# First block of two transformer blocks: scores written in alternation between row groups, compression weights used unsplit in column groups, planner given new durations

## The chip, the cores and the metric

The kernel runs on one core of one Trainium2 chip. The metric is device time in microseconds (us), the median of the runs shown; lower is better. The engines are named as in the profile: PE (TensorE; PEld is its weight load), DVE (VectorE), ACT (ScalarE), POOL (GpSimd) and SP (SyncE, which issues the DMAs).

## The reference

Two layers of a first block, then two layers of a second block, on 256 tokens of width 1024, all in fp32. The first block's layer has a sparse attention whose keys and values are, among other things, compressed. What the change touches is this:

```python
def compress(t, pe, w1, b1, w2, b2):            # once for keys, once for values, per layer
    ...
    flat = blocks.transpose(...).reshape(B, nc, G, CMP_LEN * D)     # 15 blocks x 2 groups = 30 rows of 2048
    h = jax.nn.gelu(flat @ w1 + b1)                                 # w1 is 2048 x 256
    return h @ w2 + b2
...
s_s = jnp.einsum('bqgrd,bgqkd->bgrqk', qb, k_g) * scale             # 8 heads of depth 64, in 2 groups of 4
s_w = jnp.einsum('bqgrd,bkgd->bgrqk', qb, kwb) * scale              # the same queries, windowed keys
```

With 256 tokens the selection keeps every block, so selected and windowed attention are both causal attention, with different keys and values. Projections, a gated MLP, a convolutional feed-forward part and the second block (pooling, gated linear attention, latent attention, feed-forward) follow.

## The kernel before

The program is recorded first and emitted afterwards. Every operation goes to a recorder as one `Op`; a list scheduler (`schedule`) then simulates the five engines with the durations of `_cost`, takes at each step the ready operation of lowest priority number, and so fixes the order of every engine's queue. The priority is the position in the program plus a number from the table `SHIFT`, by phase and group; the table `ALT` moves single operations to another engine (a copy from ACT to DVE, an elementwise operation from DVE to POOL and back). On the chip each engine runs its queue in this order and waits on semaphores. Since every operation is emitted from one line (L522 before, L534 after), the profile tells operations apart by tile names: `wh`/`wl` are the two parts of a weight tile, `raw` the tile as it came by DMA, `x` the split activations, `u` general tiles, and `pa`, `pb`, `upp`, `trp` PSUM tiles, two buffers of each, one bank a buffer.

A matmul on large weights is done in three: the weights are split into a rounded part and a remainder (`split`: `wh` by a copy, `wl` by a subtraction), the activations too, and high x high, high x low and low x high are summed in PSUM. Small matmuls (scores, products with the values, transposes) are plain fp32; an fp32 matmul that is not a transpose shows as two instructions, one for each of two passes.

`first_mix(i)` is the first part of a layer. `weave` interleaves generators: `compress_g(kv)` runs beside input projections, `attend_g(t)` (t is the half of the tokens, 128 each) beside the gated MLP's projections and the compressed attention.

- `compress_g`: 16 steps m of 128 rows each. For each it multiplies `xs_[:, m]` (30 columns high, 30 low) by `lv` and `hv`, two matmuls of 256 columns per step, all into one PSUM tile `trp`. Rows 0 to 29 and 30 to 59 of the result are then added by a product with the constant `pair_sum` (60 rows), once for each half of the 256 hidden values.
- `attend_g`: for t = 0 two heads share a PSUM tile `upp` (128 queries x 2 heads x 2 kinds x 128 keys), for t = 1 one head fills it. A head's score has a depth of 64, that is rows 0 to 63 of the array for the first four heads (g = 0) and rows 64 to 127 for the others (g = 1). Behind each score stands a bf16 matmul that adds the causal mask, over all 128 rows.

Of the kernel before, what the change touches and what calls it, by code (L numbers as in the profile page):

```python
# [174 lines left out]
class Recorder:  # L175
# [14 lines left out]

    def mask(self, lz):
# [115 lines left out]
def _cost(eng, meth, args, kw, reads, writes):  # L307
# [209 lines left out]
def emit(nc, order):  # L517
    for op in order:
# [9 lines left out]
        (0, 0): 11, (0, 2): -701  # L528
    },
# [5 lines left out]
    },  # L535
# [5 lines left out]
    },  # L541
    "f1m": {
        (1, 0): -520, (1, 1): -3630, (1, 2): -723, (2, 0): -251, (2, 1): 188, (2, 2): -699
    },
# [11 lines left out]
    },  # L556
# [82 lines left out]
        (0, 0): 76, (0, 2): 156  # L639
    },  # L640
    "s2": {
        (0, 0): 185
    },
}
HOLD = {
# [1366 lines left out]
```

## Time and profile before

| | |
|---|---|
| median of 3 runs (lowest, highest) | 1585.4 us (1585.31, 1591.89) |
| span of the profiled execution | 1583.9 us |
| what lies around the span, by the median | 1.5 us |
| busy: PE, PEld | 1562.3 us (99%), 1358.9 us (86%) |
| busy: DVE, ACT, POOL | 1083.7 us (68%), 761.7 us (48%), 492.3 us (31%) |
| DMA | 270.60 MB, 171 GB/s in the mean |

The page gives for the profiled execution its span, from the first instruction to the last; the time that the runs are measured by is a little longer. A matmul's end is modelled in the profile, so PE's durations overlap; the pace is read from the distance between starts.

### The profile page before, as it was taken

The page shows a single profiled execution, that of the slowest core. Times are in us where ns is not written, and L with a number is a line of the kernel's source. Part 1 is how long each engine was busy: PE and PEld are TensorE (multiplying, and loading weights), DVE is VectorE, ACT ScalarE, POOL GpSimd, SP SyncE. Part 2 cuts the span into 40 slices and gives each one's busy share as a digit, 9 for nine tenths or more (in the row PEclk, how much of TensorE's full clock was granted, in tenths as well). Part 3 has the DMA queues.
Part 4 walks back from the last instruction along what each step waited for, and adds up shares of the span by engine and source line. Part 5 has one row for each costly group of instructions (what it writes and reads, how often), then busy time and mean ns, then how long its engine had stood idle before and what let it go on. Part 6 is the DMA issues. An engine that isn't in the chain of part 4 may idle for free.

```text
span 1583.9 us, 24617 instructions
## 1 busy us (share of the span) xinstructions
PE 1562.3 (99%) x9421; PEld 1358.9 (86%) x9421; DVE 1083.7 (68%) x1582; ACT 761.7 (48%) x1333; POOL 492.3 (31%) x428
## 2 busy tenths in 40 slices
PE   7999999999999999999999999999999999999998
PEld 6778999988778999988888888999988888889997
DVE  6777877888777877886645647566566455675664
ACT  4566555554666545556453444323354534343242
POOL 2433111122433111115233552323443326424233
PEclk9999999999999999999999999999999999999999
DMA  8643765745644656736534556566555344555571
GB/s 271 221 147 103 216 186 176 217 129 172 202 128 129 211 180 189 211 121 194 180 109 132 166 186 193 172 188 188 163 183 186 107 139 160 193 173 174 178 224 38
DMA packets 264091, 270.60 MB, mean 171 GB/s; under 512 B 11698, under 2 KB 196645, under 8 KB 263973
## 3 DMA queue, kind: packets, MB, share of 16 engines
q1 hardware_dynamic: 263972, 269.03, 55.0%
q8 instruction: 74, 1.21, 0.3%
q14 instruction: 45, 0.36, 0.1%
HBM read 267.94 MB, written 1.05 MB: 170 GB/s over the span
## 4 chain that ended last, share of the span: by engine, by line
PE 96%; DVE 2%; ACT 1%; DMA 1%; SPq 0%; issue 0%; POOL 0%; DVEq 0%; POOLq 0%; ACTq 0%
PE pa L522 36%; PE upp L522 35%; PE pb L522 19%; PE trp L522 5%; DMA raw<-in_w_in_dram 1%; DVE wl L522 1%; DVE u L522 1%; SPq L522 0%; ACT L522 0%; ACT u L522 0%; ACT junk L522 0%; DVE x L522 0%; DVE wh L522 0%; ACT x L522 0%; POOL sm L522 0%
## 5 line engine op out<-in xcount | busy, mean ns | idle before, releaser
L522 ACT CAST wh<-raw 128x1024 fp32r<-128x1024 f32 (+3 forms) x382 | 393.0, 1033 | 470.3 <-PE upp L522 234.1
L522 DVE TENSOR_TENSOR wl<-raw,wh 128x1024 fp32r<-128x1024 f32 (+3 forms) x402 | 500.5, 1257 | 119.2 <-ACT wh L522 114.5
L522 PE MATMUL upp<-x,wh 128*128 128x256 f32 x2560 | 479.3, 283 | 0.0
L522 PE MATMUL pa<-wh,x 128*128 128x512 f32 (+1 forms) x1280 | 425.9, 402 | 3.7 <-DVE x L522 2.0
L522 PEld LDWEIGHTS upp<-x,wh 128*128 128x128 f32 x2560 | 406.3, 191 | 6.2 <-ACT wh L522 0.3
L522 PE MATMUL upp<-x,wl 128*128 128x256 f32 x1280 | 361.3, 283 | 1.5 <-DVE wl L522 1.5
L522 POOL TENSOR_TENSOR wl<-raw,wh 128x1024 fp32r<-128x1024 f32 (+2 forms) x94 | 228.7, 2436 | 282.8 <-ACT wh L522 121.7
L522 PEld LDWEIGHTS pa<-wh,x 128*128 128x128 f32 x1280 | 236.7, 189 | 53.2 <-ACT u L522 2.6
L522 PE MATMUL pa<-wl,x 128*128 128x512 f32 (+1 forms) x640 | 251.9, 401 | 0.0
L522 PEld LDWEIGHTS upp<-x,wl 128*128 128x128 f32 x1280 | 244.6, 191 | 3.4 <-DVE wl L522 2.0
L522 POOL TENSOR_TENSOR u<-u,u 128x256 f32<-128x256 f32 (+4 forms) x98 | 109.3, 1117 | 328.0 <-ACT u L522 288.0
L522 DVE CAST wh<-raw 128x1024 fp32r<-128x1024 f32 (+3 forms) x114 | 89.3, 787 | 100.3 <-PE pa L522 38.7
L522 PE MATMUL pb<-wh,x 128*128 128x512 f32 (+2 forms) x496 | 157.4, 384 | 0.0
L522 PEld LDWEIGHTS pa<-wl,x 128*128 128x128 f32 x640 | 120.8, 189 | 21.4 <-DVE u L522 0.8
L522 DVE TENSOR_TENSOR u<-upp,u 128x512 f32<-128x512 f32 x80 | 55.2, 690 | 72.4 <-PE upp L522 71.6
L522 PEld LDWEIGHTS pb<-wh,x 128*128 128x128 f32 x496 | 90.4, 188 | 15.8 <-ACT wh L522 0.6
L522 PE MATMUL pb<-wl,x 128*128 128x512 f32 (+2 forms) x248 | 92.2, 381 | 0.0
L522 PE MATMUL trp<-c_ident,u 128*128 128x128 f32 (+4 forms) x415 | 79.5, 274 | 2.6 <-DMA u<-in_pre_mix_g_dram 1.9
L522 POOL TENSOR_TENSOR sm<-sm,c_nhalf 128x1 f32<-128x1 f32 (+1 forms) x60 | 47.9, 799 | 106.3 <-DVE sm L522 104.3
L522 DVE SCALAR_TENSOR_TENSOR u<-u,c_cols_conv_w,u 128x254 f32<-128x254 f32 (+1 forms) x176 | 73.5, 478 | 0.0
L522 ACT ACTIVATE u<-u 128x256 f32<-128x256 f32 (+1 forms) x100 | 44.5, 445 | 55.5 <-DVE u L522 49.6
L522 POOL TENSOR_TENSOR al<-u,ah 128x256 fp32r<-128x256 f32 x22 | 22.6, 1027 | 148.0 <-ACT ah L522 78.0
(209 smaller groups left out, 2092.3 us busy)
## 6 DMA issues: line engine op xcount, KB each, us to landing
raw<-in_w_in_dram SPq DMA_DIRECT2D x112, 512.0 KB, 4.0
raw<-in_w_up_dram SPq DMA_DIRECT2D x88, 512.0 KB, 4.2
raw<-in_w_ffn_gu_dram SPq DMA_DIRECT2D x88, 512.0 KB, 4.8
raw<-in_w_down_dram SPq DMA_DIRECT2D x44, 512.0 KB, 4.4
raw<-in_w_ffn_down_dram SPq DMA_DIRECT2D x44, 512.0 KB, 4.1
raw<-in_w_o_dram SPq DMA_DIRECT2D x32, 512.0 KB, 4.0
raw<-in_cmp_w_dram SPq DMA_DIRECT2D x16, 512.0 KB, 4.9
raw<-in_w_ple_gate_dram SPq DMA_DIRECT2D x16, 512.0 KB, 3.9
```

Of the source, the lines that this page charges most:

```text
L522: f(*args, **kw)
```

## The change

Four things change in the program, and the order of everything is planned anew.

1. `attend_g` makes two score tiles `SS[0]`, `SS[1]` at a time, one for each g, and writes the scores in the order g = 0, g = 1, for t = 0 twice. The masks of both tiles are written behind them. `rec.together` makes the planner place a score only when both tiles have a bank.
2. `compress_g` no longer splits weights or activations. Step m is one fp32 matmul of 32 columns (30 and two of zeros), with result rows 32r to 32r + 31 for r = m mod 4.
3. The four partial results are added by a `pair_sum` of 128 rows, which is four unit matrices one above the other.
4. `_cost` has other durations for PE; nearly all numbers of `SHIFT` and `ALT` are replaced. Of 496 weight remainders (`wl`), 94 were made on POOL; now there are 480, of which 184 are made on POOL.

```diff
+    def together(self, op, lz):
+        t = lz.tile
+        if t not in op.tiles:
+            op.tiles.append(t)
+            t.ops.append(op)
...
         if meth == "transpose":
-            return 107.0, None
+            return 106.5, None
...
-            d = 2 * max(2 * c / 2.4, 107.0)
+            d = 2 * max(2 * c / 2.4, 107.0) + 2.5
+            if args[1].shape[-1] <= 32 and rhs.shape[0] == 128 and c == 256:
+                d = 130.0
+            elif rhs.shape[0] == 64:
+                d = 2 * c / 2.4 + 110.0
+            elif rhs.shape[0] < 64:
+                d += 190.0
         elif rhs.dtype == F32R:
-            d = c / 2.4 if c >= 256 else 4 * c / 2.4
+            d = c / 2.4 + 10.8 if c >= 256 else 4 * c / 2.4
...
 SHIFT = {
     "c1": {
-        (0, 0): 11, (0, 2): -701
+        (0, 0): -537, (0, 2): -2513
...
-    c["pair_sum"] = np.concatenate([np.eye(30, dtype=f), np.eye(30, dtype=f)], axis=0)
+    c["pair_sum"] = np.concatenate([np.eye(32, 30, dtype=f)] * 4, axis=0)
...
-            xs_ = X4.tile([128, 16, 2, 30])
-            Xm = X[:, :480].rearrange("p (m n) -> p m n", m=16)
-            nc.scalar.copy(xs_[:, :, 0], Xm)
-            nc.vector.tensor_tensor(xs_[:, :, 1], Xm, xs_[:, :, 0].bitcast(F32), op=ALU.subtract)
-            yield
...
-                    hv, lv = split(load(w1[:, m0:m0 + 4]))
-                    for mm in range(4):
-                        m = 8 * mq + 4 * mh + mm
-                        if m > 0:
-                            nc.tensor.matmul(ps1[:30, :256], xs_[:, m, 0], lv[:, mm], start=False, stop=False)
-                        nc.tensor.matmul(ps1[:60, :256], xs_[:, m].rearrange("p a n -> p (a n)"), hv[:, mm],
-                                         start=(m == 0), stop=(m == 15))
...
+            for mq in range(4):
+                raw = load(w1[:, 4 * mq:4 * mq + 4])
+                for r in range(4):
+                    nc.tensor.matmul(ps1[32 * r:32 * r + 32, :256], X[:, 4 * mq + r], raw[:, r], start=(mq == 0),
+                                     stop=(mq == 3))
+                yield
...
-                for e in range(nh):
-                    nc.tensor.matmul(S[:, e], qT[t][gp, j0 + e], kT[gp, :, 0:(t + 1) * 128], start=True, stop=False)
-                    mask_add(S[:, e, :, t * 128:(t + 1) * 128], 2)
...
+            for j0 in range(0, 4, nh):
+                SS = [bank(upp, "S").rearrange("p (e b n) -> p e b n", e=nh, b=2) for g in range(2)]
                 for e in range(nh):
+                    for g in range(2):
+                        gp = slice(g * 64, (g + 1) * 64)
+                        op = nc.tensor.matmul(SS[g][:, e], qT[t][gp, j0 + e], kT[gp, :, 0:(t + 1) * 128],
+                                              start=(e == 0), stop=False, skip_group_check=True)
+                        rec.together(op, SS[1 - g])
+                for g in range(2):
+                    S, h0 = SS[g], 4 * g + j0
+                    for e in range(nh):
+                        mask_add(S[:, e, :, t * 128:(t + 1) * 128], 2, skip_group_check=True)
```

Where the rows stand now is shown at three places. The first is PE's queue at the first scores of the first layer (t = 0). A score is `upp<-u,u 128x256`, a mask `upp<-c_causal_b,c_ident_b`. Before:

```order
L522 MATMUL pa_224<-wh_69,x_78 128x512
L522 MATMUL upp_227<-u_85,u_88 128x256
L522 LDWEIGHTS c_ident_b_196
L522 MATMUL upp_227<-c_causal_b_195,c_ident_b_196 128x256
L522 MATMUL upp_227<-u_85,u_88 128x256
L522 LDWEIGHTS c_ident_b_196
L522 MATMUL upp_227<-c_causal_b_195,c_ident_b_196 128x256
L522 MATMUL upp_228<-u_85,u_88 128x256
```

After, at the same place:

```order
L534 MATMUL pa_224<-wh_66,x_77 128x512
L534 MATMUL upp_227<-u_88,u_87 128x256
L534 MATMUL pa_224<-wl_71,x_77 128x512
L534 MATMUL upp_228<-u_88,u_87 128x256
L534 MATMUL pa_224<-wh_66,x_78 128x512
L534 MATMUL upp_227<-u_88,u_87 128x256
L534 MATMUL upp_228<-u_88,u_87 128x256
L534 LDWEIGHTS c_ident_b_196
L534 MATMUL upp_227<-c_causal_b_195,c_ident_b_196 128x256
```

The masks have moved behind the scores, and two projection matmuls (`pa`) stand between the first three scores; only the third and the fourth follow each other. Over both layers, the 32 scores stood in 32 separate places before, and now stand in 27: five pairs are adjacent (four with 256 columns, one with 512).

The second place is PE's queue at the compression of the keys in the first layer (all four weight pieces of 512 KB). Before, its first piece:

```order
L522 MATMUL pb_226<-wh_66,x_77 128x512
L522 MATMUL trp_230<-wh_67,x_79 60x256
L522 MATMUL trp_230<-wl_72,x_79 30x256 x2
L522 MATMUL trp_230<-wh_67,x_79 60x256
L522 MATMUL trp_230<-wl_72,x_79 30x256
```

After, all four pieces:

```order
L534 MATMUL upp_228<-wh_67,x_75 128x280
L534 MATMUL trp_229<-raw_64,u_84 32x256 x4
L534 MATMUL trp_229<-raw_59,u_84 32x256 x4
L534 MATMUL trp_229<-raw_62,u_84 32x256 x4
L534 MATMUL trp_229<-raw_58,u_84 32x256 x4
L534 MATMUL upp_227<-wl_72,x_75 128x280
```

The 32 matmuls of 60 or 30 columns have become 16 of 32 columns, without a break. For the values there are breaks: in both layers their 16 stand as 8, 1, 1 and 6, with single transposes between.

The third place is the head of SP's queue, the DMA issues in order. Before:

```order
L522 DMA raw_58<-in_w_in_dram 128x2x512
L522 DMA c_ident_190<-const_ident_dram 128x128
L522 DMA c_h_191<-in_x_dram 128x512 x4
L522 DMA u_84<-in_pre_mix_g_dram 16x128
L522 DMA raw_60<-in_w_in_dram 128x2x512
```

After:

```order
L534 DMA raw_58<-in_w_in_dram 128x2x512
L534 DMA w_179<-in_cmp_w_dram 128x2x64
L534 DMA b_181<-in_cmp_b_dram 30x64
L534 DMA raw_59<-in_w_in_dram 128x2x512
L534 DMA c_ident_190<-const_ident_dram 128x128
L534 DMA c_h_191<-in_x_dram 128x512 x4
L534 DMA u_85<-in_pre_mix_g_dram 16x128
```

Three issues, among them a second weight piece, have moved ahead of the identity matrix and the input x (`c_h`).

## Rows read from the trace of the kernel before

**Rows 1.** The page: busy time by engine, GB/s by slice, the chain that ended last.
```profile
PE 1562.3 (99%) x9421; PEld 1358.9 (86%) x9421; DVE 1083.7 (68%) x1582; ACT 761.7 (48%) x1333; POOL 492.3 (31%) x428
...
GB/s 271 221 147 103 216 186 176 217 129 172 202 128 129 211 180 189 211 121 194 180 109 132 166 186 193 172 188 188 163 183 186 107 139 160 193 173 174 178 224 38
...
PE 96%; DVE 2%; ACT 1%; DMA 1%; SPq 0%; issue 0%; POOL 0%; DVEq 0%; POOLq 0%; ACTq 0%
```

**Rows 2.** Cores: span and mean granted TensorE clock.
```profile
core 0: 1583.9 us, clock 0.999
```

**Rows 3.** The chain by time: start us, us, what, count.
```profile
1117.80 1.39 PE pa L522 x6
...
1120.55 17.27 PE upp L522 x144
```

**Rows 4.** Groups by shape, PE: stationary, moving operand, count, busy us, mean ns.
```profile
L522 PE MATMUL upp<-u,u 64*128 64x512 f32 x32 | 17.9, 640 | 0.0
...
L522 PE MATMUL trp<-wh,x 128*60 128x256 f32 x64 | 16.5, 285 | 0.9 <-DVE x L522 0.9
L522 PE MATMUL trp<-wl,x 128*30 128x256 f32 x64 | 15.6, 282 | 0.0
...
L522 PE MATMUL upp<-u,u 64*128 64x256 f32 x32 | 11.1, 428 | 0.0
```

**Rows 5.** Timeline of PE at scores of t = 0: start, us, operation.
```profile
60.42 0.70 PE L522 MATMUL upp<-u,u 64*128 64x256 f32 x2
61.27 0.70 PE L522 MATMUL upp<-u,u 64*128 64x256 f32 x2
```

**Rows 6.** Timeline of PE at a score of t = 1.
```profile
101.76 1.12 PE L522 MATMUL upp<-u,u 64*128 64x512 f32 x2
```

**Rows 7.** Timeline of PE in the compression, first piece.
```profile
35.92 0.28 PE L522 MATMUL trp<-wh,x 128*60 128x256 f32 x1
...
36.86 0.39 PE L522 MATMUL pb<-wh,x 128*128 128x512 f32 x1
```

**Rows 8.** Timeline of PE around an fp32 matmul of 30 columns.
```profile
65.52 0.40 PE L522 MATMUL pa<-wh,x 128*128 128x512 f32 x1
65.84 0.30 PE L522 MATMUL trp<-w,hT 128*30 128x64 f32 x2
...
66.41 0.63 PE L522 MATMUL pa<-wh,x 128*128 128x512 f32 x2
```

**Rows 9.** Timeline of PE around a product with pair_sum.
```profile
48.83 0.29 PE L522 MATMUL upp<-wh,x 128*128 128x280 f32 x1
49.05 0.40 PE L522 MATMUL trp<-c_pair_sum,u 60*128 60x30 f32 x2
...
49.62 0.29 PE L522 MATMUL upp<-wl,x 128*128 128x280 f32 x1
```

**Rows 10.** Timeline of PE at short fp32 matmuls over the whole array.
```profile
104.59 1.08 PE L522 MATMUL pa<-kcT,u 128*128 128x32 f32 x8
105.51 1.10 PE L522 MATMUL pa<-u,u 128*128 128x512 f32 x2
```

**Rows 11.** Timeline of all engines at the start of the program.
```profile
1.73 1.85 SPq L522 DMA_DIRECT2D c_h<-in_x_dram  x4
...
5.61 1.09 PE L522 MATMUL trp<-c_ident,c_h 128*128 128x128 f32 x4 [5.61 <-DMA c_h<-in_x_dram]
...
8.63 0.28 PE L522 MATMUL trp<-c_ident,u 16*128 16x16 f32 x1 [1.93 <-DMA u<-in_pre_mix_g_dram]
```

**Rows 12.** Timeline of PE at the second layer's compression of the keys.
```profile
389.49 0.33 PE L522 MATMUL trp<-wh,x 128*60 128x256 f32 x1 [0.94 <-DVE x L522]
```

**Rows 13.** Timeline of DVE at the same place.
```profile
386.77 1.35 DVE L522 TENSOR_TENSOR u<-trp,c_cols_cmp_pe 64x120 f32<-64x120 f32 x6
```

**Rows 14.** The page: the costliest groups, splits of weights on DVE and POOL.
```profile
L522 DVE TENSOR_TENSOR wl<-raw,wh 128x1024 fp32r<-128x1024 f32 (+3 forms) x402 | 500.5, 1257 | 119.2 <-ACT wh L522 114.5
...
L522 POOL TENSOR_TENSOR wl<-raw,wh 128x1024 fp32r<-128x1024 f32 (+2 forms) x94 | 228.7, 2436 | 282.8 <-ACT wh L522 121.7
```

More of the change, by code (lines that the diff above doesn't have):

```diff
@@ L1147, in tile_two_blocks, with mask_add @@
     nc.scalar.copy(ident_b, ident)
-    def mask_add(ps, n):
+    def mask_add(ps, n, **kw):
         if n == 1:
-            nc.tensor.matmul(ps, ident_b, causal_b, start=False, stop=True)
+            nc.tensor.matmul(ps, ident_b, causal_b, start=False, stop=True, **kw)
         else:
-            nc.tensor.matmul(ps, ident_b, bcast(causal_b.unsqueeze(1), [128, n, 128]), start=False, stop=True)
+            nc.tensor.matmul(ps, ident_b, bcast(causal_b.unsqueeze(1), [128, n, 128]), start=False, stop=True, **kw)
     def evac(dst, src):
@@ L1345, in compress_g @@
             yield
-            xs_ = X4.tile([128, 16, 2, 30])
-            Xm = X[:, :480].rearrange("p (m n) -> p m n", m=16)
-            nc.scalar.copy(xs_[:, :, 0], Xm)
-            nc.vector.tensor_tensor(xs_[:, :, 1], Xm, xs_[:, :, 0].bitcast(F32), op=ALU.subtract)
-            yield
             w1 = A["cmp_w1"][i, kv].rearrange("(m p) n -> p m n", p=128)
             ps1 = bank(trp, "cps")
-            for mq in range(2):
-                for mh in range(2):
-                    m0 = 8 * mq + 4 * mh
-                    hv, lv = split(load(w1[:, m0:m0 + 4]))
-                    for mm in range(4):
-                        m = 8 * mq + 4 * mh + mm
-                        if m > 0:
-                            nc.tensor.matmul(ps1[:30, :256], xs_[:, m, 0], lv[:, mm], start=False, stop=False)
-                        nc.tensor.matmul(ps1[:60, :256], xs_[:, m].rearrange("p a n -> p (a n)"), hv[:, mm],
-                                         start=(m == 0), stop=(m == 15))
-                        if m == 0:
-                            nc.tensor.matmul(ps1[:30, :256], xs_[:, m, 0], lv[:, mm], start=False, stop=False)
-                    yield
-            h1 = unit("h1")[:60, :256]
-            nc.scalar.copy(h1, ps1[:60, :256])
+            for mq in range(4):
[4 more added lines that the diff above has]
+                yield
+            h1 = unit("h1")[:, :256]
+            nc.scalar.copy(h1, ps1[:, :256])
             psh = bank(trp, "hps")
@@ L1417, in attend_g @@
             nh = 2 if t == 0 else 1
-            for h0 in range(0, 8, nh):
-                g, j0 = divmod(h0, 4)
-                gp = slice(g * 64, (g + 1) * 64)
-                S = bank(upp, "S").rearrange("p (e b n) -> p e b n", e=nh, b=2)
+            for j0 in range(0, 4, nh):
+                SS = [bank(upp, "S").rearrange("p (e b n) -> p e b n", e=nh, b=2) for g in range(2)]
                 for e in range(nh):
-                    nc.tensor.matmul(S[:, e], qT[t][gp, j0 + e], kT[gp, :, 0:(t + 1) * 128], start=True, stop=False)
-                    mask_add(S[:, e, :, t * 128:(t + 1) * 128], 2)
-                nm = sm("nm", 4)
-                nc.vector.tensor_reduce(nm[:, :2 * nh], S.rearrange("p e b n -> p (e b) n"), axis=AX.X, op=ALU.max,
-                                        negate=True)
-                pu = unit("P").rearrange("p (e b n) -> p e b n", e=nh, b=2)
-                for e in range(nh):
-                    for b in range(2):
-                        nc.scalar.activation(pu[:, e, b], S[:, e, b], AF.Exp, bias=nm[:, 2 * e + b:2 * e + b + 1],
-                                             accum_out=s3[:, b, h0 + e:h0 + e + 1])
-                pt = bank(trp, "pt").rearrange("p (a n) -> p a n", a=4)
-                pf = pu.rearrange("p e b n -> p (e b n)")
-                for a in range(4):
-                    nc.tensor.transpose(pt[:, a], pf[:, a * 128:(a + 1) * 128], ident)
-                pts = unit("PT").rearrange("p (a n) -> p a n", a=4)
-                evac(pts, pt)
-                for e in range(nh):
-                    hh = h0 + e
-                    for b in range(2):
-                        for kb in range(t + 1):
-                            nc.tensor.matmul(ob[b][:, hh * 64:(hh + 1) * 64], pts[:, (2 * e + b) * (t + 1) + kb],
-                                             vsrc[b](kb, g), start=(kb == 0), stop=(kb == t))
-                yield
@@ new lines, in attend_g @@
+                    for g in range(2):
[7 more added lines that the diff above has]
+                        mask_add(S[:, e, :, t * 128:(t + 1) * 128], 2, skip_group_check=True)
+                    nm = sm("nm", 4)
+                    nc.vector.tensor_reduce(nm[:, :2 * nh], S.rearrange("p e b n -> p (e b) n"), axis=AX.X,
+                                            op=ALU.max, negate=True)
+                    pu = unit("P").rearrange("p (e b n) -> p e b n", e=nh, b=2)
+                    for e in range(nh):
+                        for b in range(2):
+                            nc.scalar.activation(pu[:, e, b], S[:, e, b], AF.Exp, bias=nm[:, 2 * e + b:2 * e + b + 1],
+                                                 accum_out=s3[:, b, h0 + e:h0 + e + 1])
+                    pt = bank(trp, "pt").rearrange("p (a n) -> p a n", a=4)
+                    pf = pu.rearrange("p e b n -> p (e b n)")
+                    for a in range(4):
+                        nc.tensor.transpose(pt[:, a], pf[:, a * 128:(a + 1) * 128], ident)
+                    pts = unit("PT").rearrange("p (a n) -> p a n", a=4)
+                    evac(pts, pt)
+                    for e in range(nh):
+                        hh = h0 + e
+                        for b in range(2):
+                            for kb in range(t + 1):
+                                nc.tensor.matmul(ob[b][:, hh * 64:(hh + 1) * 64], pts[:, (2 * e + b) * (t + 1) + kb],
+                                                 vsrc[b](kb, g), start=(kb == 0), stop=(kb == t))
+                    yield
```

57 lines of the change are left out of this document (29 added, 28 removed), and 246 rows, old and new, of tables (ALT, HOLD, SHIFT).

## The prediction, made before the changed kernel ran

> **What bounds the kernel now.** I read the page first. PE is busy 99% of the span, and the chain that ended last is 96% PE; DVE, ACT and POOL are free for 32, 52 and 69% of it [rows 1]. The granted clock is 0.999 of full speed over the whole span, so that every price below is one at the 2.4 GHz level [rows 2]. The chain in order of time shows that PE is not only busy but at its pace: 144 matmuls of 256 columns on split weights start within 17.27 us, 0.12 us each, and six of 512 columns within 1.39 us, 0.23 us each [rows 3]. So the time changes by what PE's queue is shortened or lengthened, and by new waits in it. What is taken from ACT and DVE (16 pieces of compression weights are no longer split) is worth nothing as such, since PE's work covers it. The groups by shape then give the counts: 16 scores of 256 and 16 of 512 columns (two passes each), and 64 + 64 matmuls of the compression [rows 4]. The rest comes from timelines of PE at single places, read by the distance between starts.
>
> **Scores.** A score of 512 columns lasts 0.42 us longer than one of 256 [rows 5, 6]; so two passes stream 256 columns in 0.42 us and 512 in 0.84. But one score of 256 columns and its mask take 0.85 us from start to start [rows 5]. The mask is one pass over 256 columns, 0.12 us by the pace of [rows 3]. What is left, 0.31 us, is neither stream nor mask: it is paid where PE goes from a full-height matmul to one of 64 rows and back. Before, each of the 32 scores stands alone and pays it. The change does not bring all scores together: by the new queue they stand in 27 places, since other matmuls were planned between most pairs. Five times 0.31 is 1.6 us less. In the five adjacent pairs the two scores use different rows and different PSUM tiles; if they stream at the same time, four pairs save 0.42 and one 0.84 us, 2.5 in all. I take both: -4.1 us; the bounds are -1.6 (nothing streams side by side) and -4.1. The masks stay as many as they were.
>
> **Compression.** Now, eight matmuls (60 or 30 columns) start within 0.94 us [rows 7], 0.118 each, with no loss at their edges; 128 of them are 15.0 us. After, there are 64 fp32 matmuls of 32 columns, of two passes, 0.42 us of stream each. The trace has one kind of fp32 matmul that narrow, the product with w2 (30 columns). From the matmul before it to the second one behind it 0.89 us pass [rows 8]; two ordinary ones of 0.23 and two passes over 64 columns (a quarter of 0.42) leave 0.33 us, so the narrow fp32 form also pays for going in and out, which the split form of 30 columns did not [rows 7]. The new queue has 10 such stretches (16 for the keys; 8, 1, 1 and 6 for the values; twice): 3.3 us. Within a stretch four consecutive matmuls write four different 32-row parts of the result and use four different column groups. If four stream at a time, the keys take four rounds of 0.42, the values 2 + 1 + 1 + 2 rounds (the last stretch has r = 2 and r = 3 twice), 4.2 us per layer, 8.4 in all, 0.13 per matmul. That is 11.7 us against 15.0: -3.3. If none overlap, the stream is 26.9 us and the balance +15.2. No row of before shows two groups of the array at work together, so these are the bounds. I take the first, because each of the four has its own columns, its own PSUM rows and the whole height of the array, and nothing in the rows ties one to another; the planner's 130 ns is a number of the change and no evidence. The Trainium skill, "TensorE: Matmul & The Clock Gate", Part 3, section on the measured speedup against the span model, reports 3.07 times for four row tiles and 2.38 times for three column tiles. By 3.07 instead of 4 the compression would be an estimated 2.5 us dearer and the result 1578.1; no run here shows it yet.
>
> **pair_sum.** From the matmul before it to the second one behind it 0.79 us pass [rows 9]; less two ordinary ones of 280 columns (0.13 each by [rows 3]) it costs 0.53. With 128 rows it is an ordinary short fp32 matmul over the whole array; eight such passes take 0.92 us [rows 10], so two take 0.23. Eight products: -2.4 us. No overlap is needed for this, and I see no bound worth a range. The products with w2 for the keys, which stood apart before, are adjacent in both layers: two stretches fewer, -0.7.
>
> **Moved work.** Three issues are put ahead of the identity and of x on SP's queue. Four issues take 1.85 us there, and PE's first matmul waits for x until 5.61, the next for the first gains (issued behind x) until 8.63 [rows 11]. Three times 0.46 is 1.4 us later; one of the three is a piece of 512 KB, 1.9 us at the 271 GB/s of the first slice [rows 1]. On the other side this piece is then there when PE starts. I take +1.0, bounds 0 and +2. In the second layer PE waited 0.94 us for the split of the compression's input, which is gone [rows 12]. What now releases the first matmul are eight additions on DVE, of 1.35/6 us each [rows 13], 1.8 in all. PE's cover between the last transpose and that matmul is 1.6 us in the first layer (six of 512 columns, two of 280) and 2.2 in the second; with the signals, I count 0.6 us of new waits in both. Together -0.3. The other moves (90 more remainders on POOL, all of `SHIFT`) I put at 0 with ends of -6 and +8 us: PE is idle for 21.6 us of the span [rows 1, 2], 5.6 of it before its first matmul, and no more than a part of the other 16 can be planned away or doubled.
>
> **Sum.** -4.1 - 3.3 - 2.4 - 0.7 + 1.0 - 0.3 = -9.8 us on the profiled span of 1583.9, 1574.1. The median of the runs lies 1.5 us above that span, so 1575.6 us.
>
> **Rivals.**
> *In program order.* PE may not start a matmul's first pass before the second pass of the one ahead has started, and the two passes of one matmul share their group. Then neighbours overlap by one pass only: 0.21 us per matmul in the compression, 64 x 0.21 + 10 x 0.21 (the first pass of a stretch) + 3.3 = 18.8 us, +3.8; the score pairs save 1.3 instead of 2.5. The result is 1583.9, no change. For it: all PE starts in the timelines are in queue order. Against it: these rows have no two groups free at once. The Trainium skill, same page, Part 3, section "The mechanism", states that matmuls start and end strictly in program order, which is this rival if the two passes are separate matmuls to it; the trace agrees as far as starts go, by the records of the timelines.
> *No overlap at all* (slower). The 64 matmuls cost 0.42 us each, +15.2, and scores keep only 1.6 of their gain: 1596.6 us. It happens in the compression; with scores that do not overlap either, the change loses time from 0.25 us per matmul on, where I forecast 0.13. For it: every fp32 pass in the trace streams alone. Against it: the loads and streams of neighbours do overlap in ordinary matmuls, at 0.12 us with a load for each.
> *Late remainders.* POOL needs 2.44 us for a piece where DVE needs 1.26 [rows 14]. PE uses one up in 24 matmuls, 2.9 us, so POOL keeps up; but 90 more pieces go there, and eight of them late by the difference of 1.18 us eat the whole gain: 1585. Against it: the 94 before it left PE little idle.
>
> **How the numbers follow.** The forecast gets 0.72, program order 0.12, no overlap 0.08, late remainders 0.08. The forecast's own range, by the ends of the moved work, is 1568 to 1584. The range of 1567 to 1588 takes in the second and the fourth case and leaves out the third and small tails. About 0.5% (7.9 us: below 1577.5, above 1593.3) is what a measurement of this kernel can tell from no change. The forecast lies only 1.9 us under that bound, so a quarter of it counts as no change: faster 0.54 + 0.02; slower 0.07 from no overlap and 0.03 from the others; the rest, 0.34, no change.
>
> **What would show it.** The 16 matmuls of the keys' compression should pass in about 2.0 us from the start of the first to the start of what follows (3.9 in program order, 7.0 without overlap). In an adjacent pair the second score's first pass should start before the first score's last pass ends, and the pair of 512 columns should take about 1.15 us with its way in and out, not 2.3; a score behind a projection matmul should still cost what it does now. pair_sum should show passes at the 0.115 us pace. PE's first matmul should start near 7.0 us. I am wrong if PE's idle time rises by more than 6 us, with `wl` from POOL as the releaser, or if a compression matmul takes over 0.2 us.

## The result, and the profile after

The changed kernel takes 1595.7 us (1594.32 to 1598.28, five runs), 1.0061 times the time before (95% interval 1.0044 to 1.0077). The forecast was 1575.6 us, faster, with a range up to 1588; it is 0.6% slower. In the profile of one execution of 1594.32 us the span is 1592.5 us, 8.6 us more than before [rows 2]. The first lines of the page (busy time by engine; the split of the weights on POOL and DVE) and the cores' line answer to [rows 1, 2, 14]:

```profile
PE 1560.3 (98%) x9421; PEld 1348.3 (85%) x9421; DVE 1178.4 (74%) x1645; ACT 648.6 (41%) x1181; POOL 668.1 (42%) x483
...
L534 POOL TENSOR_TENSOR wl<-raw,wh 128x1024 fp32r<-128x1024 f32 (+3 forms) x184 | 453.9, 2471 | 522.1 <-ACT wh L534 228.9
...
L534 DVE TENSOR_TENSOR wl<-raw,wh 128x1024 fp32r<-128x1024 f32 (+2 forms) x296 | 389.3, 1322 | 89.2 <-ACT wh L534 84.0
```

```profile
core 0: 1592.5 us, clock 0.999
```

PE is idle for 32.2 us instead of 21.6. DVE is 95 us busier, although 106 subtractions fewer run on it: that is the first row to be puzzled by, and it leads to the cause below. Moved work alone doesn't explain it. Other operations came to DVE (66 roundings of whole weight pieces, 38 products of 256 columns), but by the mean times of before all that came and went, taken together, makes DVE's operations some 25 us shorter. The same forms of operation took some 126 us longer (both are estimates from counts and mean times by form, `--lines --by-form`).

The program's edits did what was forecast. Timeline of PE in the changed kernel, keys' compression of the first layer, what follows it, and a product with `pair_sum` (start us, us, operation; two instructions are one fp32 matmul):

```profile
38.61 1.93 PE L534 MATMUL trp<-raw,u 128*32 128x256 f32 x32 [0.72 <-DVE u L534]
40.48 0.40 PE L534 MATMUL upp<-wl,x 128*128 128x280 f32 x1
...
43.41 0.29 PE L534 MATMUL upp<-wh,x 128*128 128x280 f32 x1
43.53 0.30 PE L534 MATMUL trp<-c_pair_sum,u 128*128 128x30 f32 x2
43.80 0.53 PE L534 MATMUL upp<-wh,x 128*128 128x280 f32 x2
```

The 16 matmuls pass in 1.87 us (forecast 2.0), in the second layer without the wait of [rows 12], and `pair_sum` in 0.27 us [rows 9]. In the trace's single records four passes start within 20 ns, and the next four 0.22 us later. Counted from start to start less one ordinary pace, all compression costs 11.2 us beside its waits and cost 15.1 before, so -4.0 us (forecast -3.3); `pair_sum` -2.1 (-2.4); the products with w2 -0.4 (-0.7). Timeline of PE at scores, with the ones that stand alone first and an adjacent set last, to be read beside [rows 5, 6]:

```profile
64.55 0.70 PE L534 MATMUL upp<-u,u 64*128 64x256 f32 x2
65.18 0.49 PE L534 MATMUL pa<-wl,x 128*128 128x512 f32 x1
...
66.66 0.70 PE L534 MATMUL upp<-u,u 64*128 64x256 f32 x4
67.29 0.28 PE L534 MATMUL upp<-c_causal_b,c_ident_b 128*128 128x256 bf16 x1
```

Two scores of different row groups pass in the time of one: 0.63 us to the next start, alone or as a pair. All scores cost 26.9 us and cost 30.3 before, so -3.3 (-4.1).

So the loss is elsewhere. The table cuts the span at the last transposes of `c_h` in each norm, places that every profile has, and gives the length of each stretch before and the difference to it, after and in each experiment below (us of the profiled execution, worked out from the starts in the timelines). "Mix" is the first block's first part, "rest" its feed-forward part and what follows; the second block's two layers are taken together.

| | mix, layer 1 | rest, layer 1 | mix, layer 2 | rest, layer 2 | second block: mixes | its feed-forward | all |
|---|---|---|---|---|---|---|---|
| before (length) | 150.8 | 222.7 | 130.9 | 223.5 | 481.7 | 374.4 | 1583.9 |
| after | +1.2 | +1.7 | -4.5 | +0.8 | +2.4 | +7.1 | +8.7 |
| e1 old plan | +7.8 | +1.0 | +20.9 | +1.0 | +0.1 | +0.3 | +31.0 |
| e5 rest old | +7.9 | +5.7 | -3.0 | +3.5 | 0.0 | -0.1 | +14.1 |
| e8 replan rest | +18.9 | +3.2 | +24.6 | -0.4 | +2.3 | +8.7 | +57.3 |
| e9 second old | +2.9 | +7.7 | -4.5 | +0.1 | +0.7 | 0.0 | +6.8 |
| e13 second old | +3.7 | +1.6 | -4.1 | +0.3 | +0.7 | 0.0 | +2.3 |
| e2 118 to DVE | +4.2 | +0.8 | -4.0 | +0.3 | +4.3 | +4.3 | +9.9 |
| e10 two to DVE | +3.1 | +1.1 | -4.6 | +0.8 | +2.4 | +2.6 | +5.3 |
| e4 one group | +7.6 | +1.5 | +0.6 | +0.1 | +2.3 | +8.7 | +20.9 |
| e7 adjacent | -2.8 | +1.4 | -10.9 | +0.8 | +2.1 | +10.0 | +0.7 |
| e3 SP's head | +1.1 | +1.3 | -4.1 | +0.7 | +2.2 | +8.6 | +9.8 |
| e6 head of three queues | +3.5 | +1.2 | -4.2 | +0.5 | +2.0 | +8.6 | +11.8 |
| e11 positions | +4.7 | +1.6 | -4.6 | +0.6 | +2.3 | +10.3 | +14.9 |
| e14 constants late | +5.4 | +0.8 | -4.6 | +0.8 | +2.5 | +8.6 | +13.5 |
| e17 constants later | -1.5 | +1.9 | -4.0 | +0.4 | +2.1 | +10.1 | +9.0 |
| e15 = e7 + e13 | -4.0 | +1.1 | -10.9 | -0.4 | +0.5 | 0.0 | -13.9 |
| e18 = e15 + e17 | -6.5 | +1.5 | -9.9 | 0.0 | +0.7 | -0.1 | -14.4 |

The second layer's mix shows the program's gain, 4.5 us. The first layer's varies between executions: with the queues of the changed kernel it is +1.2 after, +3.1 in e10 and +3.7 in e13. The traces show why: the wait for `wl` listed below is 1.8 us in the profile after, and the clock stays at 1.00 behind it; it is 2.5 us in e10 and 2.0 in e13, and the granted clock from 37 to 41 us is 0.57 in both, so mostly 1.2 GHz. So single rows of this column are good to some 2.5 us only. The second block, in which no operation changed, loses 9.5 us. The view of PE's waits after (what was waited for: us in total, times, longest) says where:

```profile
PE trp L534 <- DMA c_h<-in_x_dram: 8.8, 1, 8.8
PE pa L534 <- ACT ah L534: 5.0, 2, 2.5
PE pa L534 <- ACT u L534: 2.4, 2, 1.2
PE pb L534 <- DVE wl L534: 1.8, 1, 1.8
```

The first was 5.6 us before [rows 11]; the second, once in each feed-forward part of the second block, and the fourth, in the first 40 us, were not there. The third, once in each of the second block's mixes, was half as long before (0.64 us each).

### The profile page after: what moved, and what is told of

Its sections match the earlier page's. It is cut to its first block, busy times and chain, and to the rows that moved or that the text cites. A ratio compares the mean times of both kernels' runs of the same rounds, so it can differ in the third digit from the quotient of the medians.

```text
span 1592.5 us, 24600 instructions
## 1 busy us (share of the span) xinstructions
PE 1560.3 (98%) x9421; PEld 1348.3 (85%) x9421; DVE 1178.4 (74%) x1645; ACT 648.6 (41%) x1181; POOL 668.1 (42%) x483
## 5 line engine op out<-in xcount | busy, mean ns | idle before, releaser
L534 POOL TENSOR_TENSOR wl<-raw,wh 128x1024 fp32r<-128x1024 f32 (+3 forms) x184 | 453.9, 2471 | 522.1 <-ACT wh L534 228.9
L534 ACT CAST wh<-raw 128x1024 fp32r<-128x1024 f32 (+1 forms) x298 | 307.1, 1033 | 502.3 <-PE upp L534 181.3
L534 PE MATMUL upp<-x,wh 128*128 128x256 f32 x2560 | 467.7, 283 | 1.2 <-DVE wh L534 0.7
L534 DVE TENSOR_TENSOR wl<-raw,wh 128x1024 fp32r<-128x1024 f32 (+2 forms) x296 | 389.3, 1322 | 89.2 <-ACT wh L534 84.0
L534 DVE CAST wh<-raw 128x1024 fp32r<-128x1024 f32 (+4 forms) x182 | 160.4, 884 | 83.2 <-PE pa L534 26.8
L534 DVE SCALAR_TENSOR_TENSOR u<-u,c_cols_conv_w,u 128x254 f32<-128x254 f32 (+1 forms) x176 | 94.1, 586 | 2.2 <-ACT u L534 1.3
L534 POOL TENSOR_TENSOR u<-u,u 128x256 f32<-128x256 f32 (+3 forms) x46 | 55.0, 1196 | 86.6 <-DVE u L534 53.0
L534 DVE TENSOR_TENSOR u<-u,u 128x256 f32<-128x256 f32 (+4 forms) x106 | 81.9, 774 | 8.5 <-ACT u L534 6.2
L534 PE MATMUL trp<-c_ident,u 128*128 128x128 f32 (+3 forms) x415 | 78.3, 276 | 2.6 <-DMA u<-in_pre_mix_g_dram 1.0
L534 ACT ACTIVATE u<-u,c_cols_pre_ffn_g,c_cols_conv_w 128x256 f32<-128x256 f32 x88 | 48.3, 594 | 59.6 <-DVE u L534 59.4
```

The lines of the kernel that those rows point to most:

```text
L534: f(*args, **kw)
```

## The experiments

Theory: the program gains what was forecast, and the new plan (the order and the engines) loses some 18 us, most of them in places that the edits don't touch. Rival: the edits themselves cost the time, through what they hold or hurry.

**The plan, part by part.** e1 is the changed program with all numbers of before; e5 with those of before outside setup and first mix; e8 the program of before with the new numbers outside the first mix.

> The changed program planned with the numbers of before (SHIFT, HOLD, ALT and the durations of the planner; in the first mix, where operations were added and removed, each number goes to the operation that corresponds). The results are the same. Theory (the edits of the program gain what was forecast, the new plan loses more): scores in 24 places with seven overlapping pairs -6.7 us, compression broken into 17 stretches about 0, pair_sum -2.4, the head as before: about 1576 us, 1571 to 1582. Rival (the edits themselves cost the time, through the two banks that a pair of scores must have at once, or the tiles that are held longer): no better than the changed kernel, 1592 to 1598 us.

> The changed program with its own plan in the setup and the first mix, and the numbers and durations of before in all other parts. Theory (outside the first mix nothing in the program changed, so what those parts lost, 12 us over eight stages, is the plan's alone; inside, the edits gain 4.5 us in the second layer and the head gives it back in the first): each stage outside the mixes is within 0.6 us of the kernel before, the two mixes are as in the changed kernel, together 3.3 us shorter than before; 1582.5 us, 1580 to 1585. Rival (the parts outside lose time because the shorter mix leaves other work to them): stages outside stay 3 us or more over before in the second block's feed-forward part, 1590 us or more.

> The kernel before, planned with the new numbers and the new durations outside the first mix, and with its own inside. Theory (the new plan costs there what it costs the changed kernel): the eight stages outside the mixes are longer by 12 us, half of it in the second block's feed-forward parts, with PE's wait of 2.5 us for ah twice; 1597.5 us, 1595 to 1600. Rival (the plan fits the changed program and only suffers from the changed mixes): within 3 us of before.

Measured 1613.9, 1602.5 and 1637.1 us (ratios 1.0176, 1.0093, 1.0315): all totals of the theory were missed. (e5's is in the range of its rival, but the rival named the second block's feed-forward part, which is at -0.1.) The second block behaved as the theory says: within 0.3 us of before with the old numbers, +11.0 us with the new ones. But the first block broke down wherever old numbers met the new program, or two sets of numbers met: the mix of layer 2 lost 21 us in e1 and 25 in e8, with the granted clock down to 0.81 in a stretch of e1:

```profile
450.00:480.00 30.00, 25.87 (x131) 16.61 (x129) 14.48 (x29) 14.36 (x49) 8.16 (x13) 0.81 0.25 76
```

(window, us, PE, PEld, DVE, ACT and POOL busy, clock, DMA share, GB/s.) So these totals can't decide between the theories; the numbers hold only together with the plan that leads up to them. e9 therefore leaves the first block alone, and e13 mends a flaw of e9: the second block's setup, which lies among the first block's work, keeps its new numbers.

```diff
+NEW = ('s', 'm1', 'c1', 'f1', 'f1e', 'f1m', 'p1', 's2')     # e9: without 's2'
-    op.dur, op.table = _cost(eng, meth, args, kw, reads, writes)
+    op.dur, op.table = _cost(eng, meth, args, kw, reads, writes, self.phase in NEW)
...
 # SHIFT, HOLD and ALT of all phases that are not in NEW: as in the kernel before
```

> The changed program with its own plan in the whole first block, and the numbers and durations of before in the second block alone. Theory (the second block's parts are the plan's loss, as the run with the old numbers outside the mixes showed stage by stage, and the first block is not touched): the four stages of the second block are within 0.2 us of the kernel before, 9.5 us shorter than in the changed kernel, all others as there; 1586 us, 1584 to 1589. Rival (the seam between two plans costs as much as in that run, where the first block's feed-forward part lost 4 us): 1590 us or more.

> The changed program with the numbers and durations of before in the second block's mixes and feed-forward parts alone; the setup of the second block keeps its new numbers, so that every queue of the first block is as in the changed kernel. Theory: the second block is as in the kernel before, 9.5 us shorter, and the first block as in the changed kernel; 1586 us, 1584 to 1588. Rival (the loss depends on what the first block leaves behind): 1590 us or more.

e9 took 1593.4 us (1.0042), with 6 us lost at the seam. e13 took 1587.6 us (1.0006, interval 0.9997 to 1.0014), 8.7 us under the changed kernel by the ratios, with the second block's feed-forward parts at +0.0; PE, DVE, ACT and POOL keep the changed kernel's order until 710 us, and the second block's first stage begins at 727. The rival falls for this part: the plan alone cost these 9 us.

**Why the feed-forward part waits.** Timelines of POOL, DVE, ACT and PE in the changed kernel around the first wait for `ah`:

```profile
1037.84 2.39 POOL L534 TENSOR_TENSOR wl<-raw,wh 128x1024 fp32r<-128x1024 f32 x1 [2.64 <-DVE wh L534]
1040.91 2.35 POOL L534 TENSOR_TENSOR wl<-raw,wh 128x1024 fp32r<-128x1024 f32 x1 [0.68 <-issue]
...
1038.66 2.13 DVE L534 CAST wh<-raw 128x1024 fp32r<-128x1024 f32 x1 [0.90 <-issue]
1040.70 0.68 DVE L534 TENSOR_TENSOR u<-upp,u 128x512 f32<-128x512 f32 x1
1041.86 1.68 DVE L534 TENSOR_TENSOR u<-u,u 128x256 f32<-128x256 f32 x1 [0.48 <-ACT u L534]
...
1043.58 0.40 ACT L534 CAST ah<-u 128x256 fp32r<-128x256 f32 x1 [1.75 <-DVE u L534]
...
1044.04 0.50 PE L534 MATMUL pa<-wh,ah 128*128 128x512 f32 x1 [2.49 <-ACT ah L534]
```

Read it backwards. PE waits for `ah`, ACT for `u`, and DVE took 1.68 us for a product that alone takes 0.43: it ends 0.28 us after POOL's second subtraction (1043.26). The rounding of 2.13 us, which alone takes 0.69, ends 0.56 us after POOL's first (1040.23). Each begins within one of POOL's subtractions and ends just behind it, so it seems that DVE stands still while POOL reads its two tiles; the next two runs test it. e2 puts back on DVE, in the same order, the 118 remainders outside the first mix that the kernel before had there; e10 only the two of these rows, in both layers.

```diff
     order = schedule(rec, classes)
+    for op in order:
+        if op.eng == "gpsimd" and op.key[:2] in (("f2", 692), ("f2", 719)):    # e2: a set of 47
+            op.eng = "vector"
```

> The changed kernel in its own order, but 118 weight remainders outside the first mix, which it makes on POOL and the kernel before made on DVE, are put back on DVE without planning anew (66 stay on POOL). Theory (while POOL reads two tiles, DVE's copies and its subtractions of two SBUF tiles stand still, and the chain u, ah, al in the feed-forward part comes late): the mean of al<-u,ah on DVE falls from 0.69 to under 0.5 us, PE's two waits of 2.5 us for ah are gone, the time falls by 5 to 9 us, 1587 to 1591. Rival (the order of the queues is at fault, not the engine): the waits for ah stay, 1594 to 1598; with 147 us more work on DVE it could be over 1600.

> The changed kernel, but two weight remainders of the second block's feed-forward part (in each of two layers), which POOL makes at 1037.84 and 1040.91 us, are put on DVE, without planning anew. Theory (these two hold DVE's rounding of the next piece for 2.13 instead of 0.69 us and the product u<-u,u for 1.68 instead of 0.43, and so make ah late): PE's two waits of 2.5 us for ah shrink to under 0.5 us, nothing else changes, 1590.5 us, 1588 to 1592. Rival (DVE is late here whoever makes the remainders, since it has them to make itself then): the waits stay over 1.5 us, 1594 us or more.

e10 took 1590.7 us (1.0024, 1.0015 to 1.0034), as forecast; the waits for `ah` are gone from its list. In the table they are worth 4.5 of the 7.1 us; the other 2.6 lie in no wait of PE of over 0.3 us, and their cause stays open. DVE at the same place in e10:

```profile
1039.83 0.69 DVE L534 CAST wh<-raw 128x1024 fp32r<-128x1024 f32 x1 [0.90 <-issue]
1040.44 0.69 DVE L534 TENSOR_TENSOR u<-upp,u 128x512 f32<-128x512 f32 x1
1041.61 0.43 DVE L534 TENSOR_TENSOR u<-u,u 128x256 f32<-128x256 f32 x1 [0.48 <-ACT u L534]
```

e2 took 1593.8 us (1.0043, 1.0029 to 1.0057), less gain than forecast and not clear of noise against the changed kernel: the waits for `ah` went, but the second block's mixes lost 1.9 us more than in the changed kernel, with DVE's own work there grown, and the first mix, which it doesn't touch, 3.0 us more, behind a wait for `wl` of 2.9 us and a clock of 0.57 as in e10; what is late in the second block's mixes was not followed further. Groups by shape on DVE (count, then busy us and mean ns) before, after and in e2:

```profile
L522 DVE TENSOR_TENSOR u<-upp,u 128x512 f32<-128x512 f32 x80 | 55.2, 690 | 72.4 <-PE upp L522 71.6
...
L522 DVE TENSOR_TENSOR al<-u,ah 128x256 fp32r<-128x256 f32 x66 | 27.8, 421 | 7.2 <-ACT ah L522 6.7
...
L522 DVE TENSOR_TENSOR u<-u,u 128x256 f32<-128x256 f32 x28 | 11.7, 418 | 2.6 <-ACT u L522 2.6
```

```profile
L534 DVE TENSOR_TENSOR u<-upp,u 128x512 f32<-128x512 f32 x80 | 54.7, 686 | 37.8 <-PE upp L534 37.1
...
L534 DVE TENSOR_TENSOR u<-u,u 128x256 f32<-128x256 f32 x66 | 53.3, 807 | 6.5 <-ACT u L534 6.2
L534 DVE TENSOR_TENSOR al<-u,ah 128x256 fp32r<-128x256 f32 x72 | 49.6, 692 | 10.4 <-ACT ah L534 9.8
```

```profile
L534 DVE TENSOR_TENSOR u<-upp,u 128x512 f32<-128x512 f32 x80 | 55.0, 688 | 37.4 <-PE upp L534 37.3
...
L534 DVE TENSOR_TENSOR al<-u,ah 128x256 fp32r<-128x256 f32 x72 | 32.9, 459 | 10.2 <-ACT ah L534 9.6
L534 DVE TENSOR_TENSOR u<-u,u 128x256 f32<-128x256 f32 x66 | 31.6, 480 | 9.2 <-ACT u L534 9.1
```

Operations with two SBUF inputs take up to twice as long in the mean where POOL makes 184 subtractions, and come back near their times of before where it makes 66; those with an input in PSUM keep their 0.69 us. The page of e2 has DVE at 1189.2 us and POOL at 384.7: 118 subtractions, 147 us of work at 1.25 us each, made DVE only 10.8 us busier.

**Do four column groups stream at once?** e4 lets the four matmuls of a piece write the same group.

```diff
-  nc.tensor.matmul(ps1[32 * r:32 * r + 32, :256], X[:, 4 * mq + r], raw[:, r], start=(mq == 0), stop=(mq == 3))
+  nc.tensor.matmul(ps1[32 * mq:32 * mq + 32, :256], X[:, 4 * mq + r], raw[:, r], start=(r == 0), stop=(r == 3))
```

> The changed kernel, but the four matmuls of one weight piece in the compression write the same 32 rows (group mq instead of r), in the same order; the sum over the four groups is the same result. Theory (the four column groups stream at the same time, and this is what the compression gains): each matmul streams alone, 64 times 0.42 instead of 16 rounds of 0.45; three neighbours in 16 still have different groups, so 12 to 19 us more, 1608 to 1615, and the keys' 16 matmuls take 5.5 to 7 us instead of 1.86. Rival (short stretches come from the unsplit form, not from the groups): no change, 1594 to 1598.

It took 1606.7 us (1.0128), 10.6 us more than the changed kernel by the ratios; the compression's start-to-start cost is 22.5 us instead of 12.0 with its waits, so all of the difference is there. The keys' row in e4, with the same queue:

```profile
38.52 4.59 PE L534 MATMUL trp<-raw,u 128*32 128x256 f32 x32 [0.72 <-DVE u L534]
```

4.6 instead of 1.9 us: the groups are the gain. The forecast of 12 to 19 us was too high, since neighbours of different pieces overlap more than it allowed: in the single records four pairs of passes start within 30 ns of each other at each of the three changes of group, the other passes 0.21 to 0.24 us apart. If the passes of one group come one by one, as the first four do, the next group's first matmul has then started before the last two ahead of it in the queue.

**Adjacent scores.** e7 moves each earlier score down to the last of its set, on PE's queue alone.

```diff
+    for pair, ops in score.items():          # the scores of two tiles made together
+        for op in ops[:-1]:
+            order.remove(op)
+        k = order.index(last[pair])
+        order[k:k] = ops[:-1]
```

> The changed kernel with the scores of a pair of tiles brought together on PE: each earlier score is moved down to the last of its set, so that 4, 4, 4, 4 scores of 256 and eight pairs of 512 columns stand in 12 places instead of 27. Nothing else moves. Theory (a pair costs what a single score costs, 0.83 us against 0.81 with 256 columns and 1.157 against 1.15 with 512, as read from the changed kernel): seven pairs of 512 save 1.15 us each and four sets of 256 about 0.98 each, 12 us together; what comes later for the softmax is covered by other matmuls: 1584 us, 1582 to 1588. Rival (the scores stood apart because the softmax needs the first one early): PE waits for u or for the exponentials' tiles take the gain, 1592 us or more.

It took 1586.7 us (1.0000, 0.9992 to 1.0009), 9.7 us less than the changed kernel by the ratios. The scores cost 13.9 instead of 26.9 us; four of 256 columns pass in 1.07 us:

```profile
66.42 1.14 PE L534 MATMUL upp<-u,u 64*128 64x256 f32 x8
67.49 0.28 PE L534 MATMUL upp<-c_causal_b,c_ident_b 128*128 128x256 bf16 x1
```

The softmax was not late. What is missing in the total lies in the second block: behind the same waits for `ah` the clock was lower in this profile, for some 3 us (window row as above; at 1.2 GHz for three of the five us, at 2.4 GHz for the rest; after had 1.00 there):

```profile
1033.20:1038.20 5.00, 4.99 (x17) 4.06 (x18) 0.95 (x2) 0.91 (x1) 2.37 (x1) 0.70 0.40 125
```

**The first 40 us.** e3 moves w2, b2 and the second weight piece behind the identity, x and the gains on SP; e6 does so on ACT and DVE as well; e11 moves the cast of the positions. This cast is what stands behind the wait for `wl` at 33.7 us. DVE's timeline after:

```profile
34.54 0.17 DVE L534 CAST c_pf<-c_pi 128x2 f32<-128x2 int32 x1 [4.57 <-DMA c_pi<-in_positions_dram]
34.62 1.23 DVE L534 TENSOR_TENSOR wl<-raw,wh 128x1024 fp32r<-128x1024 f32 x1
```

```diff
+    sync = [k for k, op in enumerate(order) if op.eng == "sync"]        # e3
+    late = [order[k] for k in sync[1:4]]
+    for op in late:
+        order.remove(op)
+    order[sync[10] - 3:sync[10] - 3] = late
...
+    order.insert(order.index(dve[k + 16]) + 1, dve[k])     # e11, dve[k] is the cast
```

> The changed kernel with one edit of SP's queue: w2, b2 and the second weight piece stand behind the identity, x and the first gains, as they do in the kernel before; all else as it was. Theory (three issues ahead of x cost what the start of PE shows): PE's first matmul starts at 5.6 us instead of 8.75 and the time falls by 2.5 to 3.2 us, to about 1592.7. Rival (the second weight piece is missed later by as much): the first matmul is earlier, but PE waits for wh or wl before 15 us, and the time stays within 1 us of 1595.7.

> The changed kernel with SP's queue as in the run before last at the head, and with the second weight piece's rounding on ACT and its subtraction on DVE moved behind the first x tiles. Theory (in that run the wait went from SP's queue into ACT's and DVE's, where the second piece's wh and wl stood ahead of the gains and of x): PE's first matmul at 5.5 us, the transpose behind the gains before 9.5 instead of 12.04, the first projection matmul at about 10.6 instead of 13.04, and the time falls by 2 to 3 us, to about 1593. Rival (the second weight piece itself is the bound of the first 20 us): the first projection matmul is earlier, but a wait for wh or wl behind it takes the gain, 1595 to 1597.

> The changed kernel with one instruction moved in DVE's queue: the cast of the positions (c_pf), which waits 4.57 us for its transfer at 34.5 us with a weight remainder behind it, stands 16 instructions later. Theory (PE's wait of 1.8 us at 33.7 us, shown as one for DVE's wl, is a wait for this transfer): the wait falls under 0.4 us and the time by 1.5 to 2 us, to 1594. Rival (the next transfer is as late): the wait moves to a wh or raw within 3 us, and the time stays.

Measured 1596.3, 1597.2 and 1598.5 us (1.0063, 1.0062, 1.0073): nothing gained. Each removed or shortened the wait that it was made for, and another stood in the next place. In e3 PE's first matmul starts at 5.49 us, and then (PE's waits in e3, and in e11):

```profile
PE trp L534 <- DVE c_cols_pre_mix_g L534: 4.0, 1, 4.0
```

```profile
PE upp L534 <- DVE wh L534: 3.7, 3, 3.0
```

Behind the latter the granted clock is 0.66 for 5 us, which adds to e11's loss. e14 takes nine transfers of the second block's constants out of the first 30 us, to behind the compression's weights; e17 puts them behind the output projection's first weight piece, past 100 us.

```diff
+    for op in [op for op in early if op.key[0] == "s2"]:   # transfers, and the cast behind them
+        order.remove(op)
+        order.insert(at, op)      # e14: behind the last piece of the compression; e17: first issue of f1
```

> The changed kernel, but the nine transfers of constants that only the second block needs (0.9 MB), and the cast of the positions, stand behind the compression's weights on SP instead of ahead of them. Theory (the first 40 us are bound by transfers, of which these are some 3 us at 271 GB/s): PE's waits at 33.7 and 38 us, together 2.9 us, fall under 1 us and the time by 2 to 3 us, to 1593. Rival (the order of the weight pieces on SP, not the bytes, makes the waits): the waits stay or move by a few us, 1595 to 1598.

> The changed kernel with the nine transfers of the second block's constants behind the first layer's output projection on SP, past 100 us, and the cast of the positions behind them. Theory (they were in the way of weight pieces at either earlier place): no wait at 33.7, 38 or 60 us, 2.5 us less than the changed kernel, 1593 us, 1591.5 to 1594.5. Rival (the weight pieces themselves are the bound): a wait of 2 us or more for wh or wl between 30 and 65 us, 1595 to 1598.

e14 took 1598.7 us (1.0079): the waits at 33.7 and 38 us were gone, and one of 5.05 us for `wl` stood right behind the new place, at 60.2 us. e17 took 1594.1 us (1.0049, 1.0037 to 1.0062), 1.9 us less than the changed kernel by the ratios, with no wait of over 1.1 us between 20 and 65 us. The two intervals overlap, so the time alone doesn't show this gain. In the profile the first mix is 2.7 us shorter than after, and a lower clock behind the waits for `ah`, as in e7, hides it in the total; e18 below shows it against e15 (0.9904 and 0.9930). So transfers that nobody needs yet stood ahead of weight pieces that were due; moving issues within this stretch only changes who is late.

**Together.** e12 is e9, e7 and e11; e15 is e13 and e7; e16 adds e14, e18 adds e17.

> Three of the edits together: the second block planned with the numbers of before, the scores of each set adjacent on PE, the cast of the positions later. If the parts add up: 9.0 (adjacent scores, measured) + 9.5 (second block) + 1.8 us (positions) less than the changed kernel, 1575.4 us, 1572 to 1579, faster than the kernel before. If the adjacent scores' gain and the plan's overlap: 1580 us or more.

> The run before last with the scores of each set adjacent on PE as well. If both gains are whole: 9.0 and 9.5 us less than the changed kernel, 1577 us; more, 1574, if the lower clock behind PE's waits for ah, which the run with adjacent scores showed in the second block, goes with those waits. Range 1572 to 1579. If they overlap: 1581 us or more.

> The same with the nine transfers late as well: 2 to 3 us less than the run before, 1572.5 us, 1569 to 1577, if the transfers bound the first 40 us; the same as that run within 1 us if they don't.

> The same edit on the kernel with the second block planned as before and the scores adjacent, which took 1574.1 us. Theory: 2.5 us less, 1571.5 us, 1569.5 to 1573.5. Rival: 1573.5 us or more.

e12 took 1582.0 us (0.9970), with the seam of e9 and the loss of e11 in it; e15 1574.1 (0.9930, 0.9916 to 0.9943); e16 1578.7 (0.9950), the loss of e14 again; e18 1571.1 us (0.9904, 0.9889 to 0.9919), faster than both kernels. The gains of e7, e13 and e17 add up, 9.7 + 8.7 + 1.9 = 20.3 us; by the ratios e18 is 25 us under the changed kernel. At least a part of the rest is the lower clock, which goes with the waits: the mean granted clock is 0.997 to 0.999 in the five runs of the changed kernel, and 0.999 in all four of e18.

## Why the prediction was wrong

**Scores, compression, pair_sum** were right in mechanism and nearly in size: -9.4 us measured in PE's starts against -9.8 forecast for these three. Of the two bounds the side-by-side one holds. The rival *in program order* (3.9 us for the keys' 16) is refuted by 1.87 us, and so is *no overlap* (7.0); in e4, without the four groups, the same 16 take 4.6 us. The estimate with a factor of 3.07 doesn't hold here either: a round of four takes 0.43 us, the 0.42 that one matmul streams.

**Moved work** is the step that failed. The prediction put "the other moves (90 more remainders on POOL, all of `SHIFT`)" at 0, with ends of -6 and +8 us, because PE was idle for only 21.6 us. But the idle time of before bounds what a plan can win, not what another can lose. Measured: +9.5 us in the second block, +2.4 in the rest of the first block, and 5.7 in the first layer's mix (+1.2 there, -4.5 in the second layer's), against a gain of 4.5 in each of two layers: the +8.7 of the table. That the plan makes the second block's loss is shown by e13, which takes back all of the feed-forward parts' 7.1 us and 1.7 of the mixes' 2.4. How it makes it is shown for 4.5 of the 7.1 (e10: POOL's subtractions hold DVE). What makes the 2.4 us in the rest of the first block, where no operation changed either, no run shows; of the first layer's mix e17 takes back 2.7 us in its profile, and the remainder is open.

**Late remainders** named the right engine and the wrong mechanism. POOL's pieces were in time; what was late was DVE, which they held up. The sign given, idle time over 6 us more "with `wl` from POOL as the releaser", came half true: idle +10.6 us, the releaser `ah` from ACT, two steps behind. The Trainium skill, "SBUF — State Buffer", section "Who interferes with whom", states that a DVE instruction with two SBUF inputs contends with a GpSimd instruction that reads SBUF, that one in a two-port mode, which copies and casts can enter, contends with GpSimd too, and that whoever starts first has the port for the whole instruction; the trace agrees (a rounding of 2.13 for 0.69 us, a product of 1.68 for 0.43, each ending just behind POOL's subtraction). The prediction did not draw on it. By the rows, 90 remainders of 2.44 us [rows 14] are 220 us in which DVE can be held, and DVE's operations did take some 126 us longer; the prediction should have asked of each chain over DVE what covers it.

**The head** was sized at +1.0 with +2 as its end. PE's first matmul came at 8.75 us, not 7.0, and the first projection at 13.04 instead of 10.59. The term counted SP's issues and one piece's bytes at the path to x; it did not ask what else the same order delays, up to 40 us. e3 shows that the +3.1 us at the first matmul were not a price of their own: without them PE waits as long for the gains.

## What to carry to other kernels

A replanned order is a change of its own: measure it apart from the edit that it was made for, by stages that the edit doesn't touch. Here edits worth 9 us were hidden by 18 us lost elsewhere, of which 9 are shown to be the plan's, and the old plan in the second block, with the scores truly adjacent and early transfers of late constants put off, brought the program 15 us under the kernel before. Moving work to an idle engine was not free here, since DVE's operations on two SBUF tiles grew to twice their time beside it: look at the mean time of the other engine's operations, form by form. And where a wait is named after an operation, look at what that operation's queue waited for before it.

## What the runs showed of the hardware

- Four fp32 matmuls of 32 columns in four column groups stream in the time of one: a lone one has its two passes start 0.24 us apart and costs 0.70 us with its way in and out; eight of them (two rounds) cost 1.09 us and sixteen (four rounds) 1.96, so a round of four adds 0.43. With the four of a round in one group, sixteen take 4.6 us (e4).
- Two fp32 scores in the two halves of the rows cost what one does (0.83 us for a pair of 256 columns, 0.81 for one; 1.157 and 1.15 with 512). Two more, in the same halves again, add 0.43 us (1.07 for 0.63 to the next start, e7).
- A wait of 2.5 us on PE was followed by a lower granted clock in some executions (a mean of 0.70 over 5 us in e7, so partly at 1.2 GHz) and not in others (1.00 after, 2.4 GHz), at the same place and with the same queue; it makes 1.4 to 1.6 us in each of the second block's feed-forward parts.
- DVE's products and subtractions on two SBUF tiles of 256 columns took 0.42 us in the mean before, 0.69 and 0.81 with 90 more subtractions on POOL, and 0.46 and 0.48 in e2; those with an input in PSUM kept 0.69 us.
